# One weight tile for a k pair of two matrices, and more seven-product pairs in the down projection: a two-layer decoder trunk

## The chip, the cores and the metric

The kernel runs on one core of one Trainium2 chip. The metric is the time of one execution on the device in microseconds. Before the change the median of three runs is 2135.94 us (2135.59 to 2136.3). Engines: PE is TensorE (matmuls), DVE VectorE, ACT ScalarE, POOL GpSimd, SP the queue that issues most of the DMAs.

## The reference

The kernel computes a trunk of two decoder layers over 256 positions of width 2048, in float32, and a final RMSNorm. Layer 0 mixes with sliding-window attention and an mLSTM, layer 1 with forgetting attention; each layer then has a SwiGLU FFN with 5632 hidden columns:

```python
h = x
for layer in range(2):
    xn = rms_norm(h, norm_mix[layer])
    h = h + (swa_mlstm_mixer(xn, ...) if layer == 0 else forgetting_attention_mixer(xn, ...))
    xn = rms_norm(h, norm_ffn[layer])
    h = h + (silu(xn @ w_gate[layer]) * (xn @ w_up[layer])) @ w_down[layer]
return rms_norm(h, norm_final)
```

Almost all work is matrix products of a 256-row activation with float32 weights: w_in and w_out of the mixers, and w_gate, w_up (2048 x 5632) and w_down (5632 x 2048) of each FFN.

## The kernel before, in words

**Products in three matmuls.** PE multiplies rounded operands (fp32r). To keep float32 accuracy each operand is split into a rounded part hi and a remainder lo, and a product a x w is the sum of three matmuls: a_hi x w_hi, a_hi x w_lo and a_lo x w_hi (`three`, L365 to L368, and the same in `gemm`, L187 to L189). Activations are split once; weights are split as they stream in: ACT casts raw to hi (L159), DVE subtracts raw - hi to lo (L160), both in `split_chunk`. The 256 rows are two row blocks t of 128 (NT = 2); one matmul is 128 rows of k, 128 rows of the activation and 512 weight columns (NB) into one PSUM bank.

**Tiles.** A raw weight tile is CK = 2 blocks of k (128 rows each) x 512 columns, 512 KB, loaded by one DMA on SP's queue (`load_raw`, L101 to L107). The pool `wr` has 4 raw buffers, `wp` has 6 for hi and 6 for lo.

**Mixers.** `gemm` (L173 to L192) walks over k two blocks at a time. For the last `skew` chunks it sorts the work by row block, so that row block 0 ends earlier than row block 1. At the start (L112 to L115) SP loads h in four column parts; one raw tile of the first projection is put behind each of the first three parts. h is transposed on PE (L239) into xh and xl, 8 transposes for each part, and the first projection's accumulator acc0 takes four k blocks after each part.

**FFN.** `pair_group` (L373 to L435) computes two 512-column blocks at once: gate and up of one hidden block, or two neighbouring column blocks of down. Its order table lists pairs of k blocks (a pair is 2 of the 128-row blocks), each plain or mixed. A plain pair is 2 matrices x 2 k blocks x 2 row blocks = 8 products of three matmuls. A mixed pair treats the 2 x 2 x 2 products as a product of 2 x 2 block matrices and needs seven products (a Winograd scheme), 21 matmuls in place of 24. It needs sums of activation blocks (`sums_of`, L223 to L232, computed once) and sums of weight blocks: four DVE subtractions into t4 (L404 to L407), which then have to be split too (`split_plain`, L261 and L262, into ht and lt). Three of the products accumulate into four extra banks `prods` over the group, which at the end are combined with one ACT copy and four DVE additions (L430 to L434). A plain group of four banks and the four prods banks alternate between the two PSUM pools of four banks each.

`ffn` (L437 to L549) walks over the 11 hidden blocks in three parts, PARTS = (0, 3, 7, 11). Each part has one gate/up group for each hidden block (ORDER: 8 pairs, 3 mixed), then two down groups over the part's hidden rows, 6 or 8 pairs: DOWN[6] has 1 mixed pair, DOWN[8] has 2. After a gate group DVE adds prods to the plain banks (L458), ACT takes silu (L460), DVE multiplies (L462), and the result is turned by DMA and split for down by a deferred step (`join`, run in the next group at position MID or MID_DOWN). After a down group c is added to h in four operations (L544) and the plain banks too (L267). In layer 1's last part the second half of the columns is done by plain `gemm` with skew=3 on the last one, followed by the final norm.

**What sets the order.** Instructions are recorded in program order; the framework's scheduler then orders them on each engine by dependencies and its own estimates, and inserts the semaphore waits. On each engine they run strictly in that order. A buffer of a pool is reused when its last reader is done.

Of the kernel before, what the change touches and what calls it, by code (L numbers as in the profile page):

```python
# [21 lines left out]
KT = D // P  # L22
FF = 5632
NB = 512
CK = 2
EPS = 1e-5
NEG = -1.0e30

# [14 lines left out]
RAWS = 4  # L43
PARTS = (0, 3, 7, 11)


# [7 lines left out]
def trunk(  # L54
# [46 lines left out]
    def load_raw(w, k0, c0, n, pool=wr):  # L101
        raw = pool.tile([P, CK, NB], F32, tag="raw", name="raw", bufs=4 if pool is wr else RAWS)
        nc.sync.dma_start(
            raw[:, :, 0:n], w[k0 * P : (k0 + CK) * P, c0 : c0 + n].rearrange("(k p) n -> p k n", p=P)
        )
        return raw

    wi = w_in_even[0]
# [47 lines left out]
    def split_chunk(raw, n):  # L156
        hi = wp.tile([P, CK, NB], F32R, tag="hi", name="hi")
        lo = wp.tile([P, CK, NB], F32R, tag="lo", name="lo")
        latest[0] = nc.scalar.copy(hi[:, :, 0:n], raw[:, :, 0:n])  # L159
        nc.vector.tensor_tensor(  # L160
            out=lo[:, :, 0:n], in0=raw[:, :, 0:n], in1=hi[:, :, 0:n].bitcast(F32), op=ALU.subtract
        )
        return hi, lo

# [57 lines left out]
    def sums_of(pool, sh, sl, copies, full=None):  # L222
        if full is None:  # L223
            full = pool.tile([P, 2, NT, P], F32, tag="tmp", name="full")
            copies(full.rearrange("p i t q -> p i (t q)"))
        s = pool.tile([P, 4, P], F32, tag="tmp", name="s4")
        nc.vector.tensor_tensor(out=s[:, 0, :], in0=full[:, 0, 1, :], in1=full[:, 1, 1, :], op=ALU.add)
        nc.vector.tensor_tensor(out=s[:, 1, :], in0=s[:, 0, :], in1=full[:, 0, 0, :], op=ALU.subtract)
        nc.vector.tensor_tensor(out=s[:, 2, :], in0=full[:, 0, 0, :], in1=full[:, 0, 1, :], op=ALU.subtract)
# [143 lines left out]
    def pair_group(fp, par, lhs, sums, mats, order, todo=()):  # L373
        plain = [[bank(par, "acc") for _ in range(NT)] for _ in range(2)]
        todo = list(todo)
        prods = None
        kinds = [kind for kind, _ in order]
        t0, t1 = slice(0, P), slice(P, 2 * P)
        for pos, (kind, pair) in enumerate(order):
            k0 = 2 * pair  # L380
            if not kind:
                last = pos == len(order) - 1
                walk = [(i, t) for i in range(CK) for t in range(NT)]
                if last:
                    walk.sort(key=lambda it: it[1])
                for m, (w, c0) in enumerate(mats):
                    hi, lo = load_chunk(w, k0, c0, NB)
                    run_due(todo, pos)
                    for i, t in walk:
                        ah, al = lhs(k0 + i)  # L390
                        ts = slice(t * P, (t + 1) * P)
                        three(
                            plain[m][t], ah[:, ts], al[:, ts], hi[:, i, :], lo[:, i, :],
                            pos == 0 and i == 0, last and i == CK - 1,
                        )
# [9 lines left out]
            nc.vector.tensor_tensor(out=t4[:, 1, :], in0=rb[:, 1, :], in1=rb[:, 0, :], op=ALU.subtract)  # L405
# [5 lines left out]
            ht, lt = [], []  # L411
            for i in range(2):
                hs = fp.tile([P, 2, NB], F32R, tag="ht", name="ht")
                ls = fp.tile([P, 2, NB], F32R, tag="lt", name="lt")
                split_plain(hs, ls, t4[:, 2 * i : 2 * i + 2, :])
                ht += [hs[:, 0, :], hs[:, 1, :]]
                lt += [ls[:, 0, :], ls[:, 1, :]]
            sh, sl = sums(pair)
            xa, la = lhs(k0)
            xb, lb = lhs(k0 + 1)  # L420
            three(prods[0], xa[:, t0], la[:, t0], hg[:, 0, :], lg[:, 0, :], first, last)
            three(plain[0][0], xb[:, t0], lb[:, t0], hg[:, 1, :], lg[:, 1, :], False, False)
            three(plain[1][0], sh[:, 3, :], sl[:, 3, :], hu[:, 1, :], lu[:, 1, :], False, False)
            three(prods[1], sh[:, 0, :], sl[:, 0, :], ht[0], lt[0], first, last)
            three(prods[2], sh[:, 2, :], sl[:, 2, :], ht[1], lt[1], first, last)
            three(prods[3], sh[:, 1, :], sl[:, 1, :], ht[2], lt[2], first, last)
            three(plain[0][1], xb[:, t1], lb[:, t1], ht[3], lt[3], False, False)
        c = fp.tile([P, 4, NB], F32, tag="c", name="c", bufs=1)
        u2 = fp.tile([P, NB], F32, tag="tmp", name="u2")
        nc.scalar.copy(c[:, 0, :], prods[0])  # L430
        nc.vector.tensor_tensor(out=u2, in0=prods[3], in1=c[:, 0, :], op=ALU.add)
        nc.vector.tensor_tensor(out=c[:, 1, :], in0=prods[2], in1=u2, op=ALU.add)
        nc.vector.tensor_tensor(out=c[:, 2, :], in0=prods[1], in1=u2, op=ALU.add)
        nc.vector.tensor_tensor(out=c[:, 3, :], in0=prods[1], in1=c[:, 1, :], op=ALU.add)  # L434
        return plain, c  # L435

    def ffn(layer, fp, sx, sd, key, idx_next=None, key_next=None, finish=None):  # L437
# [6 lines left out]
        for g0, g1 in zip(PARTS, PARTS[1:]):  # L444
# [82 lines left out]
            for n0 in (0, 2):  # L527
                if end and idx_next is None and n0 == 2:
                    for n in (2, 3):
                        acc = new_acc()  # L530
                        gemm(acc, m_of, wd, n * NB, NB, 0, nk, nk, skew=3 if n == 3 else 1)
                        close(acc, n)
                    continue
                plain, c = pair_group(
                    fp, 1 - n0 // 2, m_of, sums_d, [(wd, n0 * NB), (wd, (n0 + 1) * NB)], order, todo
                )
                todo = []
                if end and idx_next is None:
                    gf = fp.tile([P, D], F32, tag="t4", name="gf", bufs=1)
                    nc.gpsimd.dma_start(gf, norm_final.partition_broadcast(P))  # L540
                for m in range(2):
                    for t in range(NT):
                        o = h[:, t, (n0 + m) * NB : (n0 + m + 1) * NB]
                        nc.vector.tensor_tensor(out=o, in0=c[:, 2 * m + t, :], in1=o, op=ALU.add)  # L544
                for m in range(2):
                    close(plain[m], n0 + m)

# [428 lines left out]
```

## Time and profile before

| | |
|---|---|
| median of 3 runs | 2135.94 us (2135.59 to 2136.3) |
| span of the profiled execution | 2134.3 us; the runs' times lie 1.3 to 2.0 us above this span |
| PE busy | 2118.0 us, 99% |
| DVE busy | 1665.9 us, 78% |
| ACT busy | 1235.5 us, 58% |
| DMA | 418.84 MB, mean 196 GB/s |

The page gives busy times per engine over the whole span; a busy share is an average over stages that differ (the FFN keeps DVE much busier than the mixers do). Windows give the same columns for a stretch of the span. In a row of the waits the numbers are the sum of the waits in us, how many there were, and the longest. In a row of the timeline the first number is the start in us from the span's start, the second the duration. A group's row gives line, engine, operation, output <- inputs, shape, count, then busy us and the mean in ns, then the idle time before it and what ended it.

### The profile page before, as it was taken

The numbers are of one execution on the slowest core, as the hardware profiler recorded it, in microseconds if no ns is written. First come the engines' busy times: TensorE is split into PE (matmuls) and PEld (weight loads), VectorE is DVE, ScalarE is ACT, GpSimd is POOL, SyncE is SP. The second block draws the span as 40 slices with busy tenths as digits, with TensorE's granted clock in tenths as the row PEclk, the third lists the DMA queues.
The fourth block names the chain that finished last, engine by engine and source line by source line (L and its number), as shares of the span: only waits on it lengthen the run. The fifth ranks groups of instructions, "written<-read, shape, count | busy, mean of one in ns | idle before, by whom it ended". The sixth has DMA issues, their size and how long they took to land.

```text
span 2134.3 us, 26801 instructions
## 1 busy us (share of the span) xinstructions
PE 2118.0 (99%) x9772; PEld 1758.6 (82%) x9772; DVE 1665.9 (78%) x2116; ACT 1235.5 (58%) x1564; POOL 40.4 (2%) x61
## 2 busy tenths in 40 slices
PE   8999999999999999999999999999999999999998
PEld 7888888888888888888888888888888888888886
DVE  6665567998899988998745554768998998889984
ACT  6565455665567646666645544556754667556753
POOL 2010000000000000000010000000000000000000
PEclk9999999999999999999999999999999999999999
DMA  8444556666667666776575564655756666656753
GB/s 268 149 151 145 174 183 206 214 210 194 200 205 223 212 206 193 236 210 191 152 236 168 168 178 141 234 185 174 246 187 215 207 207 199 234 188 207 227 198 128
DMA packets 257060, 418.84 MB, mean 196 GB/s; under 512 B 56256, under 2 KB 64544, under 8 KB 256672
## 3 DMA queue, kind: packets, MB, share of 16 engines
q1 hardware_dynamic: 256256, 413.40, 61.1%
q0 software_dynamic: 624, 3.72, 0.5%
q8 instruction: 76, 1.25, 0.2%
q14 instruction: 56, 0.46, 0.1%
q10 hardware_dynamic: 48, 0.02, 0.0%
HBM read 404.48 MB, written 2.11 MB: 191 GB/s over the span
## 4 chain that ended last, share of the span: by engine, by line
PE 98%; ACT 1%; issue 0%; DMA 0%; DVE 0%; POOLq 0%; POOL 0%; DVEq 0%; ACTq 0%
PE acc L367 17%; PE acc L368 17%; PE acc L366 17%; PE acc L187 10%; PE acc L188 10%; PE acc L189 10%; PE prod L368 4%; PE prod L367 4%; PE prod L366 4%; PE pt L239 1%; PE p L290 1%; PE ptm L273 1%; PE po L341 1%; PE pp L333 0%; PE p L283 0%
## 5 line engine op out<-in xcount | busy, mean ns | idle before, releaser
L159 ACT CAST hi<-raw 128x1024 fp32r<-128x1024 f32 (+1 forms) x692 | 705.7, 1033 | 681.2 <-PE acc L368 308.4
L160 DVE TENSOR_TENSOR lo<-raw,hi 128x1024 fp32r<-128x1024 f32 (+1 forms) x692 | 820.4, 1198 | 317.9 <-ACT hi L159 316.3
L367 PE MATMUL acc<-lo,xh 128*128 128x512 f32 x946 | 368.1, 389 | 0.0
L368 PE MATMUL acc<-hi,xl 128*128 128x512 f32 x946 | 366.8, 389 | 0.0
L366 PE MATMUL acc<-hi,xh 128*128 128x512 f32 x946 | 366.4, 389 | 0.0
L187 PE MATMUL acc<-hi,xh 128*128 128x512 f32 (+3 forms) x736 | 276.6, 377 | 0.8 <-ACT hi L159 0.8
L189 PE MATMUL acc<-hi,xl 128*128 128x512 f32 (+3 forms) x736 | 276.6, 376 | 0.0
L188 PE MATMUL acc<-lo,xh 128*128 128x512 f32 (+3 forms) x736 | 276.3, 375 | 0.0
L368 PEld LDWEIGHTS acc<-hi,xl 128*128 128x128 f32 x946 | 177.6, 188 | 36.8
L367 PEld LDWEIGHTS acc<-lo,xh 128*128 128x128 f32 x946 | 177.6, 188 | 36.8
L366 PEld LDWEIGHTS acc<-hi,xh 128*128 128x128 f32 x946 | 177.6, 188 | 36.8
L262 DVE TENSOR_TENSOR lt<-t,ht 128x1024 fp32r<-128x1024 f32 x168 | 199.6, 1216 | 3.6 <-ACT ht L261 3.6
L367 PE MATMUL acc<-lo,mh 128*128 128x512 f32 x514 | 200.3, 390 | 0.0
L366 PE MATMUL acc<-hi,mh 128*128 128x512 f32 x514 | 200.1, 389 | 0.0
L368 PE MATMUL acc<-hi,ml 128*128 128x512 f32 x514 | 198.6, 389 | 0.0
L261 ACT CAST ht<-t 128x1024 fp32r<-128x1024 f32 x168 | 175.0, 1053 | 23.2 <-PE acc L368 13.1
L187 PEld LDWEIGHTS acc<-hi,xh 128*128 128x128 f32 x736 | 138.8, 189 | 24.9 <-ACT hi L159 1.2
L189 PEld LDWEIGHTS acc<-hi,xl 128*128 128x128 f32 x736 | 139.1, 189 | 24.3 <-issue 0.8
L188 PEld LDWEIGHTS acc<-lo,xh 128*128 128x128 f32 x736 | 139.1, 189 | 24.1 <-issue 0.7
L187 PE MATMUL acc<-hi,mh 128*128 128x512 f32 x320 | 125.8, 393 | 1.2 <-ACT mh L261 1.2
L188 PE MATMUL acc<-lo,mh 128*128 128x512 f32 x320 | 125.7, 393 | 0.0
L189 PE MATMUL acc<-hi,ml 128*128 128x512 f32 x320 | 124.0, 390 | 0.0
(306 smaller groups left out, 2768.4 us busy)
## 6 DMA issues: line engine op xcount, KB each, us to landing
raw<-in_w_gate_dram SPq DMA_DIRECT2D x176, 512.0 KB, 4.1
raw<-in_w_up_dram SPq DMA_DIRECT2D x176, 512.0 KB, 4.5
raw<-in_w_down_dram SPq DMA_DIRECT2D x176, 512.0 KB, 4.6
raw<-in_w_in_odd_dram SPq DMA_DIRECT2D x88, 512.0 KB, 3.8
raw<-in_w_in_even_dram SPq DMA_DIRECT2D x64, 512.0 KB, 3.8
raw<-in_w_out_even_dram SPq DMA_DIRECT2D x32, 512.0 KB, 3.5
raw<-in_w_out_odd_dram SPq DMA_DIRECT2D x32, 512.0 KB, 3.9
raw<-in_w_in_odd_dram SPq DMA_DIRECT2D x8, 272.0 KB, 2.9
```

What stands on the lines that cost most here:

```text
L159: latest[0] = nc.scalar.copy(hi[:, :, 0:n], raw[:, :, 0:n])
L160: nc.vector.tensor_tensor(out=lo[:, :, 0:n], in0=raw[:, :, 0:n], in1=hi[:, :, 0:n].bitcast(F32), op=ALU.subtract)
L187: nc.tensor.matmul(o, ah[:, ts], hi, start=(k == 0), stop=False)
L188: nc.tensor.matmul(o, ah[:, ts], lo, start=False, stop=False)
L189: nc.tensor.matmul(o, al[:, ts], hi, start=False, stop=(k == k_all - 1))
L239: nc.tensor.transpose(pt[:, i, t, :], h[:, t, k * P : (k + 1) * P], ident)
L261: nc.scalar.copy(dst_h, src)
L262: nc.vector.tensor_tensor(out=dst_l, in0=src, in1=dst_h.bitcast(F32), op=ALU.subtract)
L273: nc.tensor.transpose(pt[:, i, :], s_, ident)
L366: nc.tensor.matmul(o, ah, hi, start=start, stop=False)
L367: nc.tensor.matmul(o, ah, lo, start=False, stop=False)
L368: nc.tensor.matmul(o, al, hi, start=False, stop=stop)
```

## The change

The raw, hi and lo tiles become 4 blocks of 512 columns (CK = 4, 1 MB of raw, still filled by two 512 KB DMAs), and the pools get half as many buffers: `wr` 2, `wp` 3. In `gemm` a tile holds four k blocks. In `pair_group` a tile holds the k pair of both matrices, so a plain pair is one cast and one subtraction of 2048 elements per partition in place of two of 1024.

In a mixed pair three of the four raw blocks are split in one cast and one subtraction of 1536 elements (before: 1024, and 512 by `split_plain`). Two of the weight sums are one subtraction with a broadcast operand into td, the other two overwrite blocks of raw; that turns one sign, hence the change in `sums_of`. ht and lt are one tile each with one buffer (before two half-size buffers), td has one buffer, mixed raw tiles have two.

Down groups get one more mixed pair each: DOWN[6] has 2 of 6, DOWN[8] has 3 of 8, at other positions. At the start, two raw tiles of 1 MB are put behind the first two parts of h (before: three of 512 KB behind the first three). The final gemm has skew=2 (8 k blocks sorted by row block, before 6). c is added to h in one operation of 2048 elements per partition. Lines behind the loader move down by about ten.

```diff
-CK = 2
+CK = 4
+PK = 2
 DOWN = {
-    6: ((0, 0), (0, 1), (1, 2), (0, 3), (0, 4), (0, 5)),
-    8: ((0, 0), (0, 1), (0, 3), (1, 2), (0, 4), (1, 5), (0, 6), (0, 7)),
+    6: ((0, 0), (0, 1), (1, 2), (0, 3), (1, 4), (0, 5)),
+    8: ((0, 0), (1, 1), (0, 2), (1, 3), (0, 4), (1, 5), (0, 6), (0, 7)),
 }
-    wp = ctx.enter_context(tc.tile_pool(name="wp", bufs=6))
-    wr = ctx.enter_context(tc.tile_pool(name="wr", bufs=4))
+    wp = ctx.enter_context(tc.tile_pool(name="wp", bufs=3))
+    wr = ctx.enter_context(tc.tile_pool(name="wr", bufs=2))
+    def load_pair(pool, mats, k0):
+        raw = pool.tile([P, CK, NB], F32, tag="raw", name="raw", bufs=2)
+        for half, (w, c0) in zip((PK, 0), mats):
+            fetch(raw[:, half : half + PK, :], w, k0, c0, NB)
         return raw
-        if n < 3:
+        if n < 2:
             ahead.append(load_raw(wi, n * CK, OFF_KS, NB))
...
-                for m, (w, c0) in enumerate(mats):
-                    hi, lo = load_chunk(w, k0, c0, NB)
+                hi, lo = split_chunk(load_pair(wr, mats, k0), NB)
...
-            ra, rb = (load_raw(w, k0, c0, NB, fp) for w, c0 in mats)
-            hg, lg = split_chunk(ra, NB)
+            raw = load_pair(fp, mats, k0)
+            hg, lg = split_chunk(raw[:, 1:4, :], NB)
             run_due(todo, pos)
-            t4 = fp.tile([P, 4, NB], F32, tag="t4", name="t4", bufs=1)
-            nc.vector.tensor_tensor(out=t4[:, 0, :], in0=rb[:, 0, :], in1=ra[:, 0, :], op=ALU.subtract)
-            nc.vector.tensor_tensor(out=t4[:, 1, :], in0=rb[:, 1, :], in1=rb[:, 0, :], op=ALU.subtract)
-            nc.vector.tensor_tensor(out=t4[:, 2, :], in0=rb[:, 1, :], in1=t4[:, 0, :], op=ALU.subtract)
-            nc.vector.tensor_tensor(out=t4[:, 3, :], in0=ra[:, 1, :], in1=t4[:, 2, :], op=ALU.subtract)
-            hu = wp.tile([P, CK, NB], F32R, tag="hi", name="hi")
-            lu = wp.tile([P, CK, NB], F32R, tag="lo", name="lo")
-            split_plain(hu[:, 1, :], lu[:, 1, :], rb[:, 1, :])
...
+            td = fp.tile([P, 2, NB], F32, tag="td", name="td", bufs=1)
+            nc.vector.tensor_tensor(
+                out=td, in0=raw[:, 0:1, :].broadcast_to([P, 2, NB]), in1=raw[:, 1:3, :], op=ALU.subtract
+            )
+            nc.vector.tensor_tensor(out=raw[:, 0, :], in0=raw[:, 1, :], in1=td[:, 1, :], op=ALU.subtract)
+            nc.vector.tensor_tensor(out=raw[:, 1, :], in0=raw[:, 3, :], in1=raw[:, 0, :], op=ALU.subtract)
+            ht = fp.tile([P, 4, NB], F32R, tag="ht", name="ht", bufs=1)
+            lt = fp.tile([P, 4, NB], F32R, tag="lt", name="lt", bufs=1)
+            split_plain(ht[:, 0:2, :], lt[:, 0:2, :], td)
+            split_plain(ht[:, 2:4, :], lt[:, 2:4, :], raw[:, 0:2, :])
...
-                        gemm(acc, m_of, wd, n * NB, NB, 0, nk, nk, skew=3 if n == 3 else 1)
+                        gemm(acc, m_of, wd, n * NB, NB, 0, nk, nk, skew=2 if n == 3 else 1)
...
-                for m in range(2):
-                    for t in range(NT):
-                        o = h[:, t, (n0 + m) * NB : (n0 + m + 1) * NB]
-                        nc.vector.tensor_tensor(out=o, in0=c[:, 2 * m + t, :], in1=o, op=ALU.add)
+                o = h[:, :, n0 * NB : (n0 + 2) * NB].rearrange("p t (m n) -> p m t n", m=2)
+                nc.vector.tensor_tensor(out=o, in0=c.rearrange("p (m t) n -> p m t n", m=2), in1=o, op=ALU.add)
```

More of the change, by code (lines that the diff above doesn't have):

```diff
@@ L42 @@
 MID_DOWN = 5
-RAWS = 4
 PARTS = (0, 3, 7, 11)
@@ L99, in trunk, with fetch, load_raw @@
     nc.scalar.dma_start(gn[0], norm_mix.rearrange("l (k p) -> (l k) p", p=P))
[L101 to L105, printed above, removed]
+    def fetch(raw, w, k0, c0, n):
+        m = raw.shape[1]
+        nc.sync.dma_start(raw[:, :, 0:n], w[k0 * P : (k0 + m) * P, c0 : c0 + n].rearrange("(k p) n -> p k n", p=P))
+    def load_raw(w, k0, c0, n):
+        raw = wr.tile([P, CK, NB], F32, tag="raw", name="raw")
+        for half in range(0, CK, PK):
+            fetch(raw[:, half : half + PK, :], w, k0 + half, c0, n)
+        return raw
+    def load_pair(pool, mats, k0):
+        raw = pool.tile([P, CK, NB], F32, tag="raw", name="raw", bufs=2)
+        for half, (w, c0) in zip((PK, 0), mats):
+            fetch(raw[:, half : half + PK, :], w, k0, c0, NB)
         return raw
@@ L156, in split_chunk @@
     def split_chunk(raw, n):
+        m = raw.shape[1]
         hi = wp.tile([P, CK, NB], F32R, tag="hi", name="hi")
         lo = wp.tile([P, CK, NB], F32R, tag="lo", name="lo")
[L159 removed]
+        latest[0] = nc.scalar.copy(hi[:, 0:m, 0:n], raw[:, :, 0:n])
         nc.vector.tensor_tensor(
[L161 removed]
+            out=lo[:, 0:m, 0:n], in0=raw[:, :, 0:n], in1=hi[:, 0:m, 0:n].bitcast(F32), op=ALU.subtract
         )
@@ L379, in pair_group @@
         for pos, (kind, pair) in enumerate(order):
-            k0 = 2 * pair
+            k0 = PK * pair
             if not kind:
                 last = pos == len(order) - 1
-                walk = [(i, t) for i in range(CK) for t in range(NT)]
+                walk = [(m, i, t) for m in range(2) for i in range(PK) for t in range(NT)]
                 if last:
-                    walk.sort(key=lambda it: it[1])
-                for m, (w, c0) in enumerate(mats):
-                    hi, lo = load_chunk(w, k0, c0, NB)
[L388 to L395, printed above, removed]
+                    walk.sort(key=lambda it: (it[0], it[2]))
+                hi, lo = split_chunk(load_pair(wr, mats, k0), NB)
+                run_due(todo, pos)
+                for m, i, t in walk:
+                    ah, al = lhs(k0 + i)
+                    ts = slice(t * P, (t + 1) * P)
+                    b = PK * (1 - m) + i
+                    three(
+                        plain[m][t], ah[:, ts], al[:, ts], hi[:, b, :], lo[:, b, :],
+                        pos == 0 and i == 0, last and i == PK - 1,
+                    )
                 continue
@@ L420, in pair_group @@
             xb, lb = lhs(k0 + 1)
[L421 to L427, printed above, removed]
+            three(prods[0], xa[:, t0], la[:, t0], hg[:, 1, :], lg[:, 1, :], first, last)
+            three(plain[0][0], xb[:, t0], lb[:, t0], hg[:, 2, :], lg[:, 2, :], False, False)
+            three(plain[1][0], sh[:, 3, :], sl[:, 3, :], hg[:, 0, :], lg[:, 0, :], False, False)
+            three(prods[1], sh[:, 0, :], sl[:, 0, :], ht[:, 1, :], lt[:, 1, :], first, last)
+            three(prods[2], sh[:, 2, :], sl[:, 2, :], ht[:, 0, :], lt[:, 0, :], first, last)
+            three(prods[3], sh[:, 1, :], sl[:, 1, :], ht[:, 2, :], lt[:, 2, :], first, last)
+            three(plain[0][1], xb[:, t1], lb[:, t1], ht[:, 3, :], lt[:, 3, :], False, False)
         c = fp.tile([P, 4, NB], F32, tag="c", name="c", bufs=1)
```

12 lines of the change are left out of this document (3 added, 9 removed).

## Prediction, on record before the changed kernel ran

> **What bounds the kernel now.** I read the totals first, then the chain of work that ended last:
>
> ```profile
> span 2134.3 us, 26801 instructions
> ...
> PE 2118.0 (99%) x9772; PEld 1758.6 (82%) x9772; DVE 1665.9 (78%) x2116; ACT 1235.5 (58%) x1564; POOL 40.4 (2%) x61
> ...
> PE 98%; ACT 1%; issue 0%; DMA 0%; DVE 0%; POOLq 0%; POOL 0%; DVEq 0%; ACTq 0%
> ```
>
> TensorE (PE) is 99% busy and 98% of the chain is its own work. A busy PE need not be at its peak, so next I read its waits, and then its timeline in an FFN group:
>
> ```profile
> PE pg L144 <- DMA gn<-in_norm_mix_dram: 4.1, 1, 4.1
> PE acc L187 <- ACT mh L261: 1.2, 1, 1.2
> PE pt L239 <- DMA h<-in_x_dram: 1.1, 1, 1.1
> PE acc L187 <- ACT hi L159: 0.8, 1, 0.8
> PE pp L333 <- DVE s L325: 0.2, 1, 0.2
> ```
>
> ```profile
> 868.16 0.39 PE L366 MATMUL acc<-hi,xh 128*128 128x512 f32 x1
> ...
> 878.82 0.39 PE L368 MATMUL acc<-hi,xl 128*128 128x512 f32 x1
> ```
>
> PE waited 7.4 us in all, and never at the FFN's lines 366 to 368. Between the two timeline rows lie 47 steps in 10.66 us: one matmul per 0.2268 us (the 0.39 us overlap the next). So the kernel is a count of matmuls times 0.2268 us, as long as VectorE (DVE) and ScalarE (ACT) keep delivering split weights. How near they are to failing is in the windows, two over the down groups and two over gate groups of layer 0, and in the waits:
>
> ```profile
> 753.00:795.00 42.00, 42.00 (x187) 34.78 (x186) 36.27 (x45) 19.97 (x21) 0.00 (x0) 1.00 0.63 203
> 795.00:837.00 42.00, 42.00 (x187) 34.80 (x186) 35.78 (x43) 23.24 (x25) 0.00 (x0) 1.00 0.65 210
> 837.00:881.00 44.00, 44.00 (x196) 36.45 (x195) 40.78 (x48) 28.43 (x31) 0.00 (x0) 1.00 0.66 215
> 881.00:921.00 40.00, 40.00 (x179) 33.11 (x178) 37.77 (x48) 27.31 (x30) 0.00 (x0) 1.00 0.70 215
> ```
>
> ```profile
> ACT hi L159 <- PE acc L368: 308.4, 206, 4.8
> ```
>
> The columns after the window are its length, PE, PEld, DVE, ACT, POOL (busy us and count), PE clock, DMA share and GB/s. DVE is 85 to 86% busy in the down groups and 93 to 94% in the gate groups. The wait says that ACT stands idle until PE frees a hi buffer: weights are ready early, PE is the last one. The change takes matmuls from PE, adds work to DVE, and halves the number of weight buffers while doubling their size.
>
> **The change part by part.** *Matmuls.* A mixed pair is 7 products of 3 matmuls instead of 8. The new tables hold one more mixed pair in each down group: two groups in each of three parts are six in layer 0, and five in layer 1, whose last two column blocks go through the plain gemm. 11 pairs x 3 = 33 matmuls x 0.2268 = **-7.5 us**. The order in which the changed kernel's instructions stand has just 33 512-column matmuls fewer.
>
> *VectorE and ScalarE.* Their prices are in the groups by shape:
>
> ```profile
> L160 DVE TENSOR_TENSOR lo<-raw,hi 128x1024 fp32r<-128x1024 f32 x660 | 797.7, 1221 | 298.0 <-ACT hi L159 296.6
> L159 ACT CAST hi<-raw 128x1024 fp32r<-128x1024 f32 x660 | 685.7, 1052 | 647.4 <-PE acc L368 301.5 <-PE acc L189 238.5 <-issue 44.4
> L262 DVE TENSOR_TENSOR lt<-t,ht 128x1024 fp32r<-128x1024 f32 x168 | 199.6, 1216 | 3.6 <-ACT ht L261 3.6
> L262 DVE TENSOR_TENSOR lo<-raw,hi 128x512 fp32r<-128x512 f32 x84 | 57.7, 686 | 28.2 <-ACT hi L261 27.7
> L405 DVE TENSOR_TENSOR t<-raw 128x512 f32<-128x512 f32 x84 | 57.3, 682 | 0.0
> L261 ACT CAST hi<-raw 128x512 fp32r<-128x512 f32 x84 | 52.1, 620 | 71.9 <-PE acc L368 65.1 <-ACT hi L159 3.4 <-DMA raw<-in_w_down_dram 1.7
> L544 DVE TENSOR_TENSOR h<-c,h 128x512 f32<-128x512 f32 x44 | 29.3, 680 | 0.0
> ```
>
> From 512 to 1024 elements the subtraction grows by 0.535 us and the cast by 0.432. No row has 1536 or 2048. The straight line through the two sizes (a further 1.07 us per 1024 for DVE, 0.86 for ACT) is one end; the other is two, or one and a half, of the 1024-instruction: 2.29 to 2.44 us for a subtraction of 2048, 1.76 to 1.83 for 1536, 1.92 to 2.10 for a cast of 2048. I take the line, since both sizes that are shown share one fixed part. The Trainium skill, "VectorE: DVE Perf Modes", section on the TRN2 errata, gives a fixed cost per instruction and a formula that makes 2048 elements 2291 ns and 512 elements 691 ns; the trace's 512 has 682 to 686, and no run here has 2048 yet.
>
> A plain pair was two subtractions, 2.44 us, and becomes 2.29. A mixed pair was 1.22 + 0.69 + 4 x 0.68 + 2 x 1.22 = 7.07 and becomes 1.76 + 1.22 + 2 x 0.68 + 2 x 1.22 = 6.78. A gate group (5 plain, 3 mixed) thus saves 1.6 us of durations. Instructions that stand back to back overlap by some 0.06 to 0.08 us, and there are 8 fewer: about -1.0 us net, 92% instead of 93 to 94%. A down group of eight pairs goes from 6 x 2.44 + 2 x 7.07 + 4 x 0.68 = 31.5 to 5 x 2.29 + 3 x 6.78 + 2.29 = 34.1, and with 6 fewer overlaps to about +3.1 us: 36.3 + 3.1 = 39.4 of 183 matmuls' 41.5 us, **95%**. The sums for the new pair (five short subtractions) fall into one gate group of each part. So DVE stays below PE everywhere on average, but the margin in the down groups falls from about 6 us to 2. I cost this at nothing: what hides it is that every matmul of the pairs in hand can run meanwhile. Without that cover, each us by which a lo comes late is a us of PE.
>
> *Three buffers of a whole pair.* A freed hi buffer can be read again after one cast and one subtraction: 1.05 + 1.22 = 2.3 us before, 1.92 + 2.29 = 4.2 us now, which is 19 matmuls. In the new order the number of matmuls between the last use of a buffer and the first use of the lo that goes with its next contents is 24 or more nearly everywhere (42 to 80 before), once it is 16. I followed two transitions by hand (layer 0's last part, second to third gate group, and fourth gate to first down group) with the durations above: with PE at full rate each lo, each ht/lt and each evacuated bank is ready 0.5 to 2 us ahead of its first reader. So: **0**, with very little to spare. The single ht/lt buffer is as tight: in four places 6 matmuls (1.4 us) stand between its release and the next ht, for a cast of 1.05 us.
>
> *Loads.* SP issues the same 512 KB transfers, now two for a tile.
>
> ```profile
> raw<-in_w_up_dram SPq DMA_DIRECT2D x176, 512.0 KB, 4.5
> raw<-in_w_down_dram SPq DMA_DIRECT2D x176, 512.0 KB, 4.6
> raw<-in_w_in_odd_dram SPq DMA_DIRECT2D x88, 512.0 KB, 3.8
> ```
>
> A tile of gemm is free again after a cast and a subtraction, then SP loads two halves: 3.8 us and about 1.95 for the second (the spacing at the start, below), so 4.2 + 5.75 + about 0.2 of signals = 10.2 us for a ring of two tiles, whose 48 matmuls take 10.9. It just holds. I cost it at 0.
>
> *Start.* Between the first and the second part of h now stand two weight loads instead of one.
>
> ```profile
> 5.45 1.97 PE L239 MATMUL pt<-ident,h 128*128 128x128 f32 x8 [1.08 <-DMA h<-in_x_dram]
> 8.25 1.22 PE L187 MATMUL acc<-hi,xh 128*128 128x512 f32 x2 [0.83 <-ACT hi L159]
> 9.31 1.97 PE L239 MATMUL pt<-ident,h 128*128 128x128 f32 x8
> 10.93 0.78 PE L188 MATMUL acc<-lo,xh 128*128 128x512 f32 x1
> ...
> 13.87 1.03 PE L239 MATMUL pt<-ident,h 128*128 128x128 f32 x8
> 14.66 0.71 PE L187 MATMUL acc<-hi,xh 128*128 128x512 f32 x2
> ```
>
> The two h parts came 3.86 us apart with one load between, 1.93 per transfer; with two it is 5.45 + 5.8 = 11.25. The new order puts all 16 transposes of both parts ahead of the first matmul, which starts at 11.25 + 1.97 = 13.2. Then 96 matmuls (21.8 us), the other 16 transposes (2.1) and some 0.7 us at a low rate end at 37.8. Before, 12 matmuls were done by 14.66, and 84 x 0.2268 + 1.03 end at 34.7, some 35.0 with the gaps between. **+2.8 us**; one transfer alone (+1.9) is the lower end, a later first tile +4 the upper. The rows show PE slow at first: 8 transposes take 1.97 us twice, later 1.03, with the clock column at 1.00. The Trainium skill, "TensorE: Matmul & The Clock Gate", Part 1, says that the clock starts at half and opens after about 3.4 us of sustained work, closing in idle time. By that rule the pause from 7.4 to 11.25 closes it anew and the first matmuls at 13.2 pay it; without it the start costs some +2.1.
>
> *End.* The last run of one row block is 24 matmuls instead of 18, with the other block's result hidden behind it: 0 to -0.3, I take **-0.2**.
>
> Sum: 2134.3 - 7.5 + 2.8 - 0.2 = 2129.4 span. The three runs lie 1.3 to 2.0 us above this span, the median 1.6: **2131.0 us**.
>
> **The rivals.** *A little late, PE still nearly fed.* With margins of 0.5 to 2 us per transition, some will be missed by a few tenths. 0.1 to 0.3 us in each of the FFN's 33 pair groups is 3 to 9 us: 2134 to 2140, within 0.2%; the gain is given back. For it: the new order splits the three matmuls of a block (hi, lo, xl) in over 900 places, where before it was 146, so that lo products stand behind hi products of later tiles. Against: the spare ACT time.
>
> *The ring of two tiles sets the rate; slower.* Place: the ends of groups, where three plain pairs (7, then 0 and 1) follow each other, so the third uses the tile of the first. Its two transfers (4.5 + 1.95), cast and subtraction make 10.8 us for two pairs of 10.9. Just there DVE also has the four sums of prods, the four of acc and two products, 10 x 0.68 to 0.74 = 7 us, in the same queue. Three buffers give about 6.5 us of lead (10.9 less 4.2). It decides from the point where that queue delays a subtraction beyond this lead; each us beyond is paid in every group, as DVE at 95% can't regain it. At 0.5 to 1.5 us per group, 33 groups give 16 to 50 us: 2147 to 2181, about 2156 at 0.75. For it: the wait below, long already with a ring of four tiles of half the size, and the 95%. Against: ACT waits for PE and not for loads, and DVE's saving in gate groups.
>
> ```profile
> SPq L103 <- DVE lo L160: 1282.1, 546, 10.6
> ```
>
> *The change does not do what it says* can be left out: the counts are in the order.
>
> **How the numbers follow.** PE fed, 2131 with 2128 to 2133: 0.34, of which a part lies above 2131.7. A little late, 2133 to 2140: 0.31. Slower by the ring, 2140 to 2190: 0.35. About 0.2% (4.3 us) is what a measurement of this kernel tells from no change: below 2131.7 faster 0.32, to 2140.2 same 0.32, above slower 0.36. Cases of both signs hold most, so: the likeliest alone is 2128 to 2133; the range takes in the slower case up to where about 1 in 10 is left, 2127 to 2172.
>
> **What would show it.** In the profile of the changed kernel: PE with 33 matmuls fewer, its step still 0.2268 us; its waits with no row for ACT hi, DVE lo or DVE lt above a few us (right), or tens of us at the pair group's lines (rival); DVE 94 to 95% in down windows; subtractions of 2048 at 2.29 us and casts at 1.92; first matmul at about 13.2 us. I am wrong if DVE waits for raw loads or if PE rows after L436's sums start late in each group.

## The result, and the profile after

The changed kernel takes **2157.6 us** (median of 4 runs, 2154.93 to 2158.83) against 2135.99 us before (4 runs): ratio 1.0101, 95% interval 1.0087 to 1.0115. It is slower by 1%, where 2131 was forecast as likeliest; the stated range of 2127 to 2172 holds it. The profiled execution's span grew from 2134.3 to 2155.2 us, by 20.9. Its page:

```profile
span 2155.2 us, 25131 instructions
...
PE 2119.7 (98%) x9739; PEld 1754.0 (81%) x9739; DVE 1672.8 (78%) x1696; ACT 1191.4 (55%) x1204; POOL 40.2 (2%) x61
...
PE 90%; DVE 3%; ACT 3%; DMA 2%; issue 1%; SPq 1%; ACTq 0%; POOLq 0%; POOL 0%; DVEq 0%
```

PE has 33 instructions fewer, as it should, but only 90% of the last chain is its own (98% before): the chain now runs through DVE, ACT and DMA as well. VectorE's busy share stayed at 78%. PE's waits, all of them:

```profile
PE pt L249 <- DMA h<-in_x_dram: 6.2, 2, 4.2
PE acc L376 <- ACT mh L271: 5.5, 2, 2.8
PE pt L249 <- DVE h L277: 4.9, 1, 4.9
PE pg L153 <- DMA gn<-in_norm_mix_dram: 2.9, 1, 2.9
PE acc L377 <- DVE lo L170: 2.5, 2, 1.3
PE acc L376 <- ACT hi L169: 1.4, 2, 0.8
PE acc L198 <- DVE lo L170: 1.0, 2, 0.7
PE prod L376 <- ACT ht L271: 0.9, 4, 0.2
PE acc L197 <- ACT mh L271: 0.7, 1, 0.7
PE prod L376 <- ACT hi L169: 0.4, 1, 0.4
```

26.4 us instead of 7.4. The waits are few and most of the time is in long ones, once per layer: not a little in each of 33 groups.

Where it went can be followed by landmarks: the start of the first matmul of each stage in the timelines (first projection, first FFN matmul, first down matmul of each part, last matmul). The table gives the lag behind the kernel before; the last column takes out the saved matmuls (6 for two down groups, 1.36 us, in each part, 3 in the last).

| stage that ends at | before, us | after, us | lag, us | lost in this stage, us |
|---|---|---|---|---|
| first matmul of the first projection | 8.25 | 12.99 | +4.7 | 4.7 |
| layer 0: first FFN matmul | 350.09 | 351.72 | +1.6 | -3.1 |
| part 1: first down matmul | 475.51 | 477.14 | +1.6 | 0.0 |
| part 2: first down matmul | 706.32 | 708.48 | +2.2 | 1.9 |
| part 3: first down matmul | 956.56 | 965.29 | +8.7 | 7.9 |
| layer 1: first matmul | 1042.89 | 1056.41 | +13.5 | 6.2 |
| layer 1: first FFN matmul | 1433.02 | 1447.63 | +14.6 | 1.1 |
| part 1: first down matmul | 1558.45 | 1573.00 | +14.6 | -0.1 |
| part 2: first down matmul | 1789.25 | 1804.36 | +15.1 | 1.9 |
| part 3: first down matmul | 2039.49 | 2061.09 | +21.6 | 7.9 |
| last matmul | 2124.95 | 2145.89 | +20.9 | 0.0 |

28.4 us are lost, 7.5 saved. The gate groups of the first part, where only the tiles changed, lose nothing. The later steps are mostly one place each: one stretch makes 5.0 of the 7.9 us, the wait at the end of layer 0 makes 4.9 of the 6.2, and 1.6 of the 1.9 us lie at the third plain pair. The rest of the 7.9 are stops of 0.2 to 1.1 us between 776.78 and 840.11, with waits for ht and hi.

**The join, 2.8 us twice, and the clock behind it.** After the last gate group of part 2, ACT takes silu (L465), DVE multiplies, ACT copies c into 16-bit halves (L490), SP turns them by DMA, ACT copies them back (L497) and casts mh (L271). ACT in the changed kernel, start and duration:

```profile
711.90 0.72 ACT L465 ACTIVATE c<-c,r 128x512 f32<-128x512 f32 x1 [0.36 <-DVE c L463]
715.52 1.48 ACT L169 CAST hi<-raw 128x1536 fp32r<-128x1536 f32 x1 [2.90 <-PE prod L378]
721.60 1.91 ACT L169 CAST hi<-raw 128x2048 fp32r<-128x2048 f32 x1 [4.59 <-PE acc L378]
723.41 0.72 ACT L465 ACTIVATE c<-c,r 128x512 f32<-128x512 f32 x1
724.03 3.28 ACT L169 CAST hi<-raw 128x1536 fp32r<-128x1536 f32 x2
727.21 1.05 ACT L271 CAST ht<-td 128x1024 fp32r<-128x1024 f32 x1
728.16 1.05 ACT L271 CAST ht<-raw 128x1024 fp32r<-128x1024 f32 x1
729.11 1.99 ACT L490 COPY c<-c 128x1024 uint16<-128x1024 uint16 x2
...
739.01 1.04 ACT L271 CAST mh<-c 128x1024 fp32r<-128x1024 f32 x1
```

ACT stands still for 4.59 us in front of a cast whose hi buffer PE has not yet freed; the second silu stands behind it, then two casts and both ht casts stand ahead of L490. This is how the delay looks in ACT's queue; which coarse element makes it is a question for the experiments. The copies start 20.6 us after the down group began (708.48), before 12.8 (719.08 against 706.32):

```profile
719.08 1.99 ACT L485 COPY c<-c 128x1024 uint16<-128x1024 uint16 x2
...
729.23 1.05 ACT L261 CAST mh<-c 128x1024 fp32r<-128x1024 f32 x1
```

PE in the changed kernel runs out of other work and then runs slowly:

```profile
736.61 0.73 PE L376 MATMUL prod<-ht,sd 128*128 128x512 f32 x2
740.10 0.50 PE L376 MATMUL acc<-hi,mh 128*128 128x512 f32 x1 [2.76 <-ACT mh L271]
...
741.70 0.63 PE L377 MATMUL prod<-lt,sd 128*128 128x512 f32 x1
742.13 0.63 PE L378 MATMUL prod<-ht,sd 128*128 128x512 f32 x1
```

742.13 - 741.70 = 0.43 us per matmul instead of 0.23, seven times up to 744.69. From 736.13 to 745.01 there are 17 steps in 8.88 us, 5.0 more than at 0.2268 each. The window's clock says so too, and VectorE's busy time says that it is not full where PE waits (columns as before: length, PE, PEld, DVE, ...):

```profile
706.00:750.00 44.00, 41.15 (x173) 33.28 (x172) 37.79 (x37) 25.43 (x21) 0.00 (x0) 0.96 0.67 207
```

DVE 86%, clock 0.96.

**The end of layer 0, 4.9 us.** The prods of the last down group are done late, so that their sums, c's addition to h, two lo and four additions stand one behind the other around the last matmul (1050.82); PE's transposes start at 1056.07, behind the first of the four additions. DVE in the changed kernel:

```profile
1048.07 0.69 DVE L436 TENSOR_TENSOR u<-prod,c 128x512 f32<-128x512 f32 x1 [3.01 <-PE prod L378]
...
1050.72 2.29 DVE L547 TENSOR_TENSOR h<-c,h 128x2048 f32<-128x2048 f32 x1
1052.93 2.48 DVE L170 TENSOR_TENSOR lo<-raw,hi 128x1088 fp32r<-128x1088 f32 x2
1055.33 2.48 DVE L277 TENSOR_TENSOR h<-acc,h 128x512 f32<-128x512 f32 x4
```

Before, the same first sum began at 1031.45, 11.4 us ahead of the next layer's first matmul; now it is 8.3 us ahead, of which PE waits 4.9. The 1.1 us of the next row of the table are the slow clock behind this wait: PE's 272-column matmuls come 0.23 us apart until 1058.8 and 0.125 after.

**The ring of two, 1.9 us twice.** SP issues both halves of the third plain pair's tile at 616.61 and 617.02, right after the first pair's subtraction (614.29, 2.29 us long); ACT gets them 6.06 us later, after waiting 2.76, and PE waits 1.27 for lo:

```profile
616.61 0.37 SPq L103 DMA_DIRECT2D raw<-in_w_gate_dram  x1
617.02 0.47 SPq L103 DMA_DIRECT2D raw<-in_w_up_dram  x1
```

```profile
622.67 1.91 ACT L169 CAST hi<-raw 128x2048 fp32r<-128x2048 f32 x1 [2.76 <-DMA raw<-in_w_up_dram]
```

It is the end of part 2's second gate group, into which the new tables put the sums for their first mixed pair. Run a below has the old tables, no such sums here and no wait; the sums were not tried alone.

### The profile page after: what moved, and what is told of

Read it like the earlier page. It is cut to its first block, busy times and chain, and to the rows that moved or that the text cites. A ratio compares the mean times of both kernels' runs of the same rounds, so it can differ in the third digit from the quotient of the medians.

```text
span 2155.2 us, 25131 instructions
## 1 busy us (share of the span) xinstructions
PE 2119.7 (98%) x9739; PEld 1754.0 (81%) x9739; DVE 1672.8 (78%) x1696; ACT 1191.4 (55%) x1204; POOL 40.2 (2%) x61
## 4 chain that ended last, share of the span: by engine, by line
PE 90%; DVE 3%; ACT 3%; DMA 2%; issue 1%; SPq 1%; ACTq 0%; POOLq 0%; POOL 0%; DVEq 0%
PE acc L376 15%; PE acc L377 15%; PE acc L378 15%; PE acc L198 10%; PE acc L199 10%; PE acc L197 10%; PE prod L378 4%; PE prod L377 4%; PE prod L376 3%; DVE lo L170 1%; ACT hi L169 1%; DMA raw<-in_w_up_dram 1%; PE ptm L283 1%; PE po L351 1%; PE p L300 1%
## 5 line engine op out<-in xcount | busy, mean ns | idle before, releaser
L170 DVE TENSOR_TENSOR lo<-raw,hi 128x2048 fp32r<-128x2048 f32 (+4 forms) x388 | 818.3, 2116 | 279.8 <-ACT hi L169 278.8
L169 ACT CAST hi<-raw 128x2048 fp32r<-128x2048 f32 (+4 forms) x388 | 684.0, 1770 | 502.5 <-PE acc L199 148.7
L376 PE MATMUL acc<-hi,xh 128*128 128x512 f32 x946 | 351.7, 390 | 1.4 <-ACT hi L169 1.4
L271 ACT CAST ht<-td 128x1024 fp32r<-128x1024 f32 x95 | 100.0, 1053 | 182.6 <-PE acc L378 166.7
L377 PE MATMUL acc<-lo,mh 128*128 128x512 f32 x437 | 170.3, 391 | 0.0
L376 PE MATMUL acc<-hi,mh 128*128 128x512 f32 x437 | 163.1, 392 | 5.5 <-ACT mh L271 5.5
L378 PE MATMUL acc<-hi,ml 128*128 128x512 f32 x437 | 168.2, 390 | 0.0
L272 DVE TENSOR_TENSOR lt<-td,ht 128x1024 fp32r<-128x1024 f32 x95 | 116.0, 1221 | 50.2 <-ACT ht L271 49.4
L271 ACT CAST ht<-raw 128x1024 fp32r<-128x1024 f32 x95 | 99.6, 1048 | 52.1 <-DVE raw L418 52.1
L197 PE MATMUL acc<-hi,mh 128*128 128x512 f32 x320 | 124.9, 394 | 0.7 <-ACT mh L271 0.7
L198 PE MATMUL acc<-lo,mh 128*128 128x512 f32 x320 | 125.3, 392 | 0.0
```

The lines of the kernel that those rows point to most:

```text
L169: latest[0] = nc.scalar.copy(hi[:, 0:m, 0:n], raw[:, :, 0:n])
L170: nc.vector.tensor_tensor(out=lo[:, 0:m, 0:n], in0=raw[:, :, 0:n], in1=hi[:, 0:m, 0:n].bitcast(F32), op=ALU.subtract)
L197: nc.tensor.matmul(o, ah[:, ts], hi, start=(k == 0), stop=False)
L198: nc.tensor.matmul(o, ah[:, ts], lo, start=False, stop=False)
L271: nc.scalar.copy(dst_h, src)
L272: nc.vector.tensor_tensor(out=dst_l, in0=src, in1=dst_h.bitcast(F32), op=ALU.subtract)
```

## The experiments

Theory 1 at first: coarse tiles alone cost about 28 us by such collisions, the tables are worth 7.5. The rival: the tables overload VectorE. Times are medians; the ratio is to the kernel before, run on the same chip. Each edit also gives the scheduler another order to find, so a difference is that of the edit and its order together.

**a, the changed kernel with the old tables.**

```diff
-    6: ((0, 0), (0, 1), (1, 2), (0, 3), (1, 4), (0, 5)),
-    8: ((0, 0), (1, 1), (0, 2), (1, 3), (0, 4), (1, 5), (0, 6), (0, 7)),
+    6: ((0, 0), (0, 1), (1, 2), (0, 3), (0, 4), (0, 5)),
+    8: ((0, 0), (0, 1), (0, 3), (1, 2), (0, 4), (1, 5), (0, 6), (0, 7)),
```

> The changed kernel with the old DOWN tables: coarse tiles alone. Theory 1 (a few collisions of coarse tiles in strictly ordered queues cost about 28 us: the start, the third plain pair of a run, the join of the last hidden block, the end of layer 0; the extra mixed pairs themselves are worth their 7.5 us): PE has 33 matmuls more than in the changed kernel and the time stays clearly above before, 2145 to 2162 us. Rival (the third mixed pair in the down groups overloads VectorE, the coarse tiles are harmless): 2136 to 2141 us, only the start is lost.

2136.27 us, ratio 1.0006 (0.9997 to 1.0015). My theory fell: coarse tiles alone cost nothing in the FFN, and hardly anything in the whole. PE's waits hold no row of the FFN:

```profile
PE pt L249 <- DMA h<-in_x_dram: 6.2, 2, 4.2
PE pg L153 <- DMA gn<-in_norm_mix_dram: 3.0, 1, 3.0
PE acc L198 <- DVE lo L170: 1.0, 2, 0.7
PE acc L197 <- ACT mh L271: 0.7, 1, 0.7
```

The lag at the first matmul is +4.8 us as in the changed kernel, at the first FFN matmul +0.2. Part of this is luck of the clock: in layer 0's mixer PE has a stretch at half rate in the kernel before and in several runs, but the traced execution of a has next to none. The rows are the kernel before, a, and i below, with clock 0.94, 1.00 and 0.93:

```profile
190.00:215.00 25.00, 25.00 (x117) 20.64 (x117) 13.84 (x18) 11.04 (x15) 0.00 (x0) 0.94 0.47 142
190.00:215.00 25.00, 25.00 (x127) 20.16 (x126) 13.79 (x25) 9.65 (x14) 0.00 (x0) 1.00 0.41 126
190.00:215.00 25.00, 25.00 (x116) 19.82 (x117) 13.89 (x27) 9.95 (x17) 0.12 (x1) 0.93 0.33 93
```

a and i have PE's instructions in the same order up to the FFN, and i is 3.6 us later there, 2.1 of it from the start and 1.6 from this stretch. Of a's ten executions seven lie at 2135.6 to 2137.0 us and three at 2139.1 to 2140.2.

**b, the kernel before with the new tables.** The new sums need 4 KB per partition more; two weight sums overwrite ra for that.

```diff
-            t4 = fp.tile([P, 4, NB], F32, tag="t4", name="t4", bufs=1)
+            td = fp.tile([P, 2, NB], F32, tag="td", name="td", bufs=1)
...
+            nc.vector.tensor_tensor(out=ra[:, 0, :], in0=rb[:, 1, :], in1=td[:, 0, :], op=ALU.subtract)
+            nc.vector.tensor_tensor(out=ra[:, 1, :], in0=ra[:, 1, :], in1=ra[:, 0, :], op=ALU.subtract)
```

> The kernel before with the new DOWN tables; two of the weight sums overwrite the raw tile, so that the larger sums fit (same instructions, same counts of buffers for hi, lo, ht, lt). Theory 1: the fine tiles carry the extra mixed pairs, 2128 to 2132 us. Rival (VectorE overloaded by the tables): 2145 us or more, with PE waits for lo or ht at the down groups.

**2128.06 us, ratio 0.9964 (0.9951 to 0.9977): faster than both kernels.** The last matmul is 7.7 us earlier, the 33 matmuls. The rival fell too; VectorE is nearly full in these down groups, and PE never waits there:

```profile
704.00:745.00 41.00, 41.00 (x183) 33.96 (x182) 39.22 (x48) 27.44 (x29) 0.00 (x0) 1.00 0.65 205
745.00:787.00 42.00, 42.00 (x187) 34.80 (x186) 40.42 (x49) 22.16 (x23) 0.00 (x0) 1.00 0.66 213
```

96% here without a wait, 86% in the changed kernel with one. So neither half costs more than a few us by itself; together they cost 29.5 us against b. What is lost is not VectorE's time; that it is lead (how long before its use a tile is ready) is the reading of the rows above.

**c, the start with one half tile behind each part of h.**

```diff
-        if n < 2:
-            ahead.append(load_raw(wi, n * CK, OFF_KS, NB))
+        if n % 2 == 0:
+            ahead.append(wr.tile([P, CK, NB], F32, tag="raw", name="raw"))
+        fetch(ahead[-1][:, n % 2 * PK : (n % 2 + 1) * PK, :], wi, n * PK, OFF_KS, NB)
```

> The changed kernel with one 512 KB half tile behind each part of h, as before the change. Theory 1: the second 8 transposes start at about 9.3 us instead of 11.4, and 1.5 to 3 us of the whole go: 2154.6 to 2156. Rival (what the start loses is made up by the first layer's mixer, as the lead of 4.7 us at the first matmul was only 1.6 us at the FFN): 2157 to 2158.

2159.61 us, ratio 1.011 (1.0095 to 1.0125). Above both expectations. The second transposes do start at 8.58 us, but the first cast needs both halves of its tile, and the order put 24 transposes ahead of the first matmul, at 14.01. In the FFN of layer 0 every loss returns in place and size (part 2 to part 3: lag +2.9 to +9.5), so a shift of the start doesn't move them.

**d, ht and lt as half tiles with two buffers.**

```diff
-            ht = fp.tile([P, 4, NB], F32R, tag="ht", name="ht", bufs=1)
-            lt = fp.tile([P, 4, NB], F32R, tag="lt", name="lt", bufs=1)
+                hs = fp.tile([P, 2, NB], F32R, tag="ht", name="ht", bufs=2)
+                ls = fp.tile([P, 2, NB], F32R, tag="lt", name="lt", bufs=2)
```

> The changed kernel with ht and lt as two half tiles with two buffers, as before the change. If the single ht/lt buffer holds up the last mixed pair of a group (at the end of layer 0 the third pair's cast waited 3.4 us for PE): the wait of 4.9 us at the end of layer 0 shrinks to under 2 and the total to 2148 to 2154. If the order of the queues is the cause and not this buffer: 2155 to 2160, the two waits of 2.8 us for mh still there.

2144.97 us, ratio 1.0042 (1.0025 to 1.0059): 12.6 us come back, more than expected, though the wait at the end of layer 0 is still 2.5 instead of under 2 us. The joins of part 2 are in time; waits of 0.5 us for mh and 1.5 for ml are left in layer 0's last part, one of 4.0 for mh in layer 1's:

```profile
PE acc L376 <- ACT mh L271: 4.5, 2, 4.0
PE pt L249 <- DVE h L277: 2.5, 1, 2.5
```

The traced execution is the slowest of the four (2149.26 us). The hi buffers are those of the changed kernel here, so they alone don't make part 2's joins late.

**e, c added to h in four operations.** The loop of the kernel before in place of the one operation of 2048 elements.

> The changed kernel with c added to h in four operations of 512 as before, nothing else. Theory: the one operation of 2048 delays h at the end of layer 0 by under 2 us only; what is late there are the prods, ready 3.0 us before the end instead of 11. So 2155 to 2158, the wait there 3 to 5 us. Rival: the wait falls under 1.5 us and the total to 2152 or less.

2147.2 us, ratio 1.0053 (1.0036 to 1.0069). My expectation fell, the rival's holds: 10.4 us come back, and the wait for h at the end of layer 0 is gone. Waits for mh of 4.1 us in all are left.

**f, L490's copies on POOL.**

```diff
-                    nc.scalar.copy(flat[:, b, :, :], cu[:, 0:2, :, b])
+                    nc.gpsimd.tensor_copy(flat[:, b, :, :], cu[:, 0:2, :, b])
```

> The changed kernel with the two copies that split c into 16-bit halves (the first step of the join) on POOL instead of ACT. Theory: in the changed kernel those copies start 20.6 us after the last gate group's end (12.8 before) because ACT's queue stands in front of them, so mh comes 2.8 us too late in both layers, with a slow clock behind each wait. With the copies on the idle POOL the two waits for mh shrink or go and 4 to 12 us come back: 2146 to 2154. Rival (ACT is late anyway, the copies only follow): the waits stay and the time is 2156 to 2160.

2175.22 us, ratio 1.0184 (1.0169 to 1.02), slower still and above both expectations. The copies of part 2 start at 737.36, 19.4 us after the down group began (20.6 in the changed kernel): silu stands behind a cast that waits 5.02 us for PE, so ACT is late anyway, as the rival said. One copy takes 2.28 us on POOL and 1.04 on ACT. PE's waits for mh fall from 5.5 to 2.6 us, but 6.2 for lt, 3.9 for ht and 4.4 for c stand in the FFN now.

```profile
L490 POOL COPY c<-c 128x1024 uint16<-128x1024 uint16 x40 | 90.2, 2282 | 1169.3 <-DVE c L467 1169.3
```

**h, the three mixed pairs at positions 2, 4 and 5.** DOWN[8] = (0,0), (0,1), (1,2), (0,3), (1,4), (1,5), (0,6), (0,7).

> The changed kernel with the three mixed pairs of DOWN[8] at positions 2, 4 and 5 instead of 1, 3 and 5, the same count. Theory: at position 1 the first mixed pair's casts stand in ACT's queue ahead of the previous gate group's end and its join; one position later the waits for mh go, 2140 to 2150; the end of layer 0 keeps its 4.9 us or gets worse. Rival (it is the count of mixed pairs, not their place): 2154 to 2162.

2169.26 us, ratio 1.0154 (1.0139 to 1.0169). A miss, above both expectations. PE's waits for mh do fall, from 5.5 to 2.6 us, but with two mixed pairs side by side PE waits 6.2 us for ht (0.9 in the changed kernel), so this run doesn't tell what position 1 costs.

**i, two mixed pairs of eight, at positions 1 and 3.** DOWN[8] = (0,0), (1,1), (0,2), (1,3), then plain; DOWN[6] as before the change.

> The changed kernel with two mixed pairs of eight (positions 1 and 3 instead of 3 and 5) and one of six, so PE has as many matmuls as before. If the third mixed pair is what breaks the coarse tiles: 2134 to 2140, as with the old tables (2136). If the early place at position 1 is: 2145 to 2160 with waits for mh.

2138.36 us, ratio 1.001 (1.0001 to 1.0019). From the first FFN matmul (lag +3.8) to the last matmul (+3.6) nothing is lost. So position 1 with two mixed pairs costs nothing, as positions 3 and 5 cost nothing in a: with coarse tiles the loss needs the third mixed pair (the second of six). It is not the number three by itself: the gate groups have three mixed pairs of eight too, at positions 2, 4 and 6, and lose nothing in a. That place was not tried for the down groups.

**j, two casts and two subtractions of 1024 for each tile of 2048.**

```diff
+        for ms in ([slice(2, 4), slice(0, 2)] if m == 4 else [slice(0, m)]):
-        latest[0] = nc.scalar.copy(hi[:, 0:m, 0:n], raw[:, :, 0:n])
+            latest[0] = nc.scalar.copy(hi[:, ms, 0:n], raw[:, ms, 0:n])
...
```

> The changed kernel with two casts and two subtractions of 1024 for each tile of 2048, in the same tiles and buffers. If long instructions are the cause (a lo comes 2.3 us late instead of 1.2, silu waits behind a long cast): 2128 to 2140. If the coarse buffers are (a hi buffer comes free only with the whole pair, and ACT's queue stands behind that wait): 2148 to 2162, with VectorE busier by some 40 us over the span.

2146.35 us, ratio 1.0049 (1.0034 to 1.0064): between the two expectations, 11.3 us come back. The wait for h at the end of layer 0 stays at 4.9 us, those for mh sum to 5.0 in four pieces of at most 1.4.

**k_de and k_dej, the undoings together.** d and e in one kernel; then with j.

> The changed kernel with both single undoings that gained most: ht and lt as half tiles with two buffers, and c added to h in four operations. If each removes a different wait, their gains of 12.6 and 10.4 us add up: 2130 to 2138. If they only shift the same tight schedule about (each gain is what any loosening gives): 2142 to 2150.

> As the run beside it, and two casts and two subtractions of 1024 for each tile of 2048: the work on VectorE and ScalarE is then cut as fine as before, only the hi, lo and raw buffers are those of a whole pair. If the length of the single operations is the cause: 2128 to 2133, the time of the fine tiles with the new tables (2128). If the coarse buffers are: above 2138, with ScalarE waiting for PE to free a hi buffer ahead of silu and of the join.

2136.34 us, ratio 1.0001 (0.9991 to 1.001), and 2134.11 us, ratio 0.9994 (0.9984 to 1.0003). d and e give 21.3 us together, 23.0 singly: they add up. j, worth 11.3 us alone, adds only 2.2 on top, within the intervals, and k_dej falls between its two expectations: what j gives back is mostly what d and e give back too. In k_de PE waits 0.5 us for lo and 0.8 for hi in the FFN, and nothing for mh, although the raw, hi and lo buffers and the casts and subtractions are as coarse as in the changed kernel. Of the 8 us that still part it from b, half (4.2) is in layer 1's mixer, where 1.9 us of waits bring a slow clock (PE in k_de):

```profile
1054.27 0.86 PE L197 MATMUL acc<-hi,xh 128*128 128x512 f32 x3 [0.79 <-ACT hi L169]
...
1056.60 0.57 PE L198 MATMUL acc<-lo,xh 128*128 128x512 f32 x1 [1.09 <-DVE lo L170]
1056.97 0.63 PE L199 MATMUL acc<-hi,xl 128*128 128x512 f32 x1
1057.40 0.63 PE L198 MATMUL acc<-lo,xh 128*128 128x512 f32 x1
...
1059.96 0.55 PE L198 MATMUL acc<-lo,xh 128*128 128x512 f32 x1
1060.35 0.39 PE L199 MATMUL acc<-hi,xl 128*128 128x512 f32 x1
```

**l, fine tiles with 3 of 6 mixed pairs**, b with DOWN[6] = (0,0), (1,1), (0,2), (1,3), (1,4), (0,5).

> The fine tiles with the new tables (2128.06 us) and one more mixed pair in DOWN[6], 3 of 6 at positions 1, 3 and 4: 12 matmuls fewer. VectorE is 91 to 96% busy there in the run with 2 of 6, and a mixed pair costs it 2.2 us more than a plain one, while the group gets 0.68 us shorter: about 98 to 101%. If fine tiles can be loaded up to the end of VectorE's time: 2125 to 2126.5. If the lead runs out before that: 2128 to 2136, with PE waits for lo or lt in the first part's down groups.

2144.91 us, ratio 1.0042 (1.0029 to 1.0056), 16.9 us above b and above both expectations. From the first down matmul of part 1 to that of part 2 the lag grows from -0.6 to +5.9 us, in layer 1 from +3.1 to +11.0; with 2.7 us saved, 9.2 and 10.6 us are lost there, and all else is as in b. Fine tiles break too, one mixed pair later, but for another reason. The expectation's 2.2 us for a mixed pair is too low: by the prediction's rows it is 7.07 - 2.44 = 4.6, and VectorE's busy time is 17.6 us above b's for four pairs. In b VectorE is busy 59.3 of the 63.5 us of these two groups; two more mixed pairs make an estimated 68.5 for 62.1 us of matmuls, 110%. By this estimate VectorE itself has too little time here, and the run says little on lead. The window is the second of these two down groups, in layer 0 (PE 26.77 of 31 us, clock 0.94; DVE is 90% busy and also waits 2.2 us for a load):

```profile
507.00:538.00 31.00, 26.77 (x108) 20.90 (x109) 27.99 (x35) 14.74 (x17) 0.00 (x0) 0.94 0.54 171
```

The pair also stands beside another mixed one here, as in h; the two were not tried apart.

## Why the prediction was wrong, step by step

*What bounds the kernel: right.* PE sets the time as long as it is fed, at 0.2268 us per matmul: b has 33 matmuls fewer and its last one is 7.7 us earlier.

*Prices: right.* The new shapes lie on the line through the old ones:

```profile
L170 DVE TENSOR_TENSOR lo<-raw,hi 128x2048 fp32r<-128x2048 f32 x277 | 634.2, 2290 | 253.6 <-ACT hi L169 252.6
L170 DVE TENSOR_TENSOR lo<-raw,hi 128x1536 fp32r<-128x1536 f32 x95 | 166.6, 1754 | 8.4 <-ACT hi L169 8.4
L169 ACT CAST hi<-raw 128x2048 fp32r<-128x2048 f32 x277 | 529.0, 1910 | 388.0 <-PE acc L199 128.6 <-PE acc L378 73.6 <-DMA raw<-in_w_up_dram 36.0
```

2.29, 1.75 and 1.91 us against 2.29, 1.76 and 1.92. The formula in the Trainium skill, "VectorE: DVE Perf Modes", section on the TRN2 errata, made it 2291 ns; the trace has 2290.

*"Three buffers of a whole pair: 0" and "I cost this at nothing": this is the step that failed.* The FFN's stages lost 25.7 us where the sum has 0. I worked by hand through two transitions, found each part 0.5 to 2 us early, and carried that over to all. Neither was among the places that broke: the join of part 2, the tail of layer 0's last down group ahead of transposes, and the third plain pair. Within the step, the buffers that were named first are not the ones that the runs accuse: k_de keeps the three hi buffers of a whole pair and loses 3 us in the FFN. The sentence at its end, on the single ht/lt buffer with 1.4 us for a cast of 1.05, names what d undoes (12.6 us), and the one addition of c to h, counted only as VectorE's time, is what e undoes (10.4). A margin that small should have been followed from part to part, with silu, join and the sums of the prods in the queues of ACT and DVE; I had counted ACT's spare time (58% busy before) as a reason against, but a strictly ordered queue can't use it when its head waits, as in the 4.59 us above.

*VectorE at 95% as the thing to fear: half right.* Fine tiles run at 96% without a wait; coarse ones wait at 86%, where 95% was forecast. Busy share did not tell which kernel would stall. What coarse tiles change is how long each buffer and queue is held: one hi buffer for a whole pair, ht for a whole mixed pair, DVE for 2.3 us at a time.

*The start: right, and then hidden.* The first matmul came at 12.99 us (13.2 forecast), and after 96 matmuls PE was 3.1 us behind (2.8 forecast). At the FFN 1.6 us was left, and 0.2 in a, to 4.3 in d. Part of that spread is the stretch at half rate shown under a, which differs although PE's order up to the FFN is the same in a and i; what sets its length stays open. The prediction let the first matmuls pay for the pause ahead of them, and the trace has transposes of 1.97 us and the first two matmuls at half rate (1.20 us for both, at 12.99) behind a wait of 4.16 us; from 14.82 on they come 0.23 us apart.

*The rivals.* For "a little late" I named the new order, which splits the three matmuls of a block in many places. Counted in successive PE rows there are 140 such places before and 688 after, not over 900; a has 488 and loses nothing in the FFN, so splitting alone isn't the cause. The ring of two has its place in the trace, but it brought only 1.9 us per layer, not 0.75 us in every group; that its 2156 us lies so near the measured time is luck. The 7.9 and 6.2 us came through mechanisms that I had not named: the join behind a waiting cast, and the additions to h behind late prods.

*The price of a wait: missed.* I counted a us of wait as a us. Here a wait of 2.8 us cost a further 1.4: seven matmuls at 0.43 us. k_de has 3.4 us at half rate after waits of 0.79 and 1.09. The rule that I had cited for the start (the Trainium skill, "TensorE: Matmul & The Clock Gate", Part 1) has the clock close after an idle window of about 3.4 us; here it closed after shorter waits, and the measurement decides.

What is shown: the extra mixed pairs pay on fine tiles; coarse tiles cost the FFN nothing with two mixed pairs; the loss needs both; undoing either of two coarse elements gives back 10 to 13 us, both nearly all of the FFN's loss. What is not: the exact share of each coarse element, since every edit also gave the scheduler another order; and whether three mixed pairs at other positions, or more hi buffers, would do as well.

## What to carry to other kernels

Merging instructions and tiles saves time on VectorE and ScalarE, but it pays only if tiles are still ready as early as before: count how long each merged tile holds its buffer and its queue, above all where an in-order engine also carries results to the next stage. Test the two halves of such a change alone: here one half gained 0.36%, and together they lost 1%. When PE is the bound, a wait of two or three us can cost half as much again, as its clock drops behind it.

## What the hardware showed unexpectedly

PE falls to half its rate (0.43 us per 512-column matmul) after some waits in the middle of a busy stage, for some 3 us, at most 6: after 2.76 us of wait the slow matmuls begin 1.6 us after PE resumed (740.10 to 741.70), after d's 3.99 us 1.1 us after it (2080.95 to 2082.05), in k_de right after the 1.09. Later than the first 16 us, all 16 waits of 2.49 us or more in these traces had such a stretch within 4 us. Of shorter ones only some had: in e one of 2.06 us did (991.51) and one of 2.05 did not (2079.84). VectorE kept PE fed at 96% busy. POOL needs 2.28 us for a strided copy of 1024 16-bit elements per partition for which ACT needs 1.04; the profile's spans on POOL are rough.
